# Three conditional regions per expert instead of four, with a longer ring of split weights and a shorter ring of raw ones

## The chip, the cores and the metric

One core of a Trainium2 chip runs the whole block as one program. The metric is the device time of that program in microseconds, the median of several runs. Engines: PE is the matrix engine (PEld its weight loads), DVE the vector engine, ACT the scalar engine, POOL GpSimd, SP the queue that issues most weight transfers. Some stretches depend on the data: the routing decides how many tokens each expert gets.

## The reference, cut to what matters

A transformer layer on 1024 tokens of width 1024: a mixer (gated DeltaNet beside sparse attention), an output projection, and then a routed feed-forward of 32 experts with 4 experts per token. All inputs are float32.

```python
logits = (h @ router_w + router_b)
top_val, top_idx = lax.top_k(logits, TOP_K); gate = softmax(top_val)
# for each expert e, the tokens routed to it, in blocks of 128 rows xb:
act = clamped_swiglu(xb @ w1[e] + b1[e])      # w1[e]: 1024 x 2048
y   = act @ w2[e] + b2[e]                     # w2[e]: 1024 x 1024
out[token] += gate * y
```

## The kernel before, in words

The last of four phases, `phase4`, is the expert feed-forward and takes about 1590 of the 2613 us. It is unrolled over the 32 experts. An expert's weights come as NS = 12 *pieces* of 1 MB (eight of w1, four of w2). `fetch` brings a piece into one of NR = 8 *raw* buffers (`self.raw[g % NR]`); four of them (the phase before has finished with `yT`) lie in the tile `yT`, so half of the weight transfers and splits are named `yT` in the trace. Each piece is cut into two *halves*, and `split` (lines 191 to 194) makes of each half a rounded part `hi` on ACT and the remainder `lo` on DVE, into a ring of NW = 10 buffer pairs. After the second half of a piece is split, the next transfer into that raw buffer is issued on SP (`fetch(g // 2 + NR)`).

A `Block` multiplies a block of tokens with a piece: per half, four matmuls with `hi` and `lo` against the rounded tokens, and two of `hi` against the tokens' remainder (line 1672). `behind(s)` does the work after a piece: `act` (lines 1714 to 1717, after pieces 1, 3, 5, 7), `turn` (a transpose, lines 1724 to 1729, after pieces 3, 5, 7, 9) and `result` (line 1734). Every expert has a `first` block of up to 128 tokens. If more came, a second block is computed in a conditional *region* (line 1530): `both` with all 128 rows if there are more than 192 tokens, else `half` with 64 rows, where `whole` (lines 1704 and 1705) first adds two halves of a PSUM bank into the tile `y1`, out of which the results are later added to the output by an indirect transfer (`add_rows`).

The 12 pieces are taken in groups of GP = 3: for each group its splits are issued, then the first block's three pieces, then one region with the second block's three pieces. So there are four regions per expert, 128 in all. The split issued LOOK = NW - 2 * GP = 4 halves ahead leaves room for the whole group's halves, which the region needs again:

```python
for s0 in range(0, NS, GP):
    group = range(s0, s0 + GP)
    for s in group:
        for part in range(2):
            split(2 * (e * NS + s) + part + LOOK)
    for s in group:
        first.room(s); first.piece(s, wt); first.behind(s)
    with tc.If(several > 0):
        ...
```

The order of the instructions on each engine is not the program's: a scheduler of the framework lists them by its own model of times. It takes a region as one unit on PE, ACT and DVE, and nothing is moved into or out of it; splits may end up behind a region that follows them in the program.

`phase3`, before it, loads the four pieces of `w_out` into raw[0] to raw[3], splits them into the first eight pairs of the ring (lines 1172 to 1175), and after each one issues the fetch of an expert piece into the freed buffer (line 1176). The other four raw buffers are fetched on ACT's queue near the end of the phase (line 1264).

Of the kernel before, what the change touches and what calls it, by code (L numbers as in the profile page):

```python
# [10 lines left out]
F32 = mybir.dt.float32  # L11
# [9 lines left out]
P = 128  # L21
# [6 lines left out]
NE = 32  # L28
# [10 lines left out]
ROWS = T + P  # L39
NS = 12  # L40
KEEP = 1
GP = 3
NR, NW = 8, 10
LOOK = NW - 2 * GP


# [90 lines left out]
class K:  # L137
# [1019 lines left out]
    def phase3(self):  # L1157
        nc, tc, A, pp = self.nc, self.tc, self.A, self.pp
# [4 lines left out]
        with ExitStack() as es:  # L1163
            hp = es.enter_context(self.pool("p3h", 1))
# [3 lines left out]
            self.rings()  # L1168
            wo = list(zip(self.hi, self.lo))
            wo += [tuple(hp.tile([P, 2, 512], F32R, name=f"{n}{i}") for n in ("wohi", "wolo")) for i in range(NW, 8)]  # L1170
            for g in range(4):
                nc.sync.dma_start(self.raw[g], A['w_out'][g])
            for g in range(4):
                for h in range(2):
                    self.split(self.raw[g][:, 2 * h:2 * h + 2], *wo[2 * g + h])
                self.fetch(g)
            it32 = hp.tile([P, NE], F32, name="it32")
            nc.gpsimd.iota(it32, pattern=[[1, NE]], base=0, channel_multiplier=0, allow_small_or_imprecise_dtypes=True)
            before = hp.tile([P, P], BF, name="before")
# [75 lines left out]
            for i in range(NT):  # L1255
# [3 lines left out]
                if i == NT - 2:  # L1259

                    self.raw += [self.yT[:, 2 * g:2 * g + 2].rearrange("p a (b c) -> p (a b) c", b=2) for g in range(4)]
                    with tc.issue_after(self.xload.ins):
                        for g in range(4, NR):
                            self.fetched = self.fetch(g, nc.scalar)
                if i == 0:

# [133 lines left out]
    def rings(self):  # L1400

        wp = self.wp

        self.lo = [wp.tile([P, 2, 512], F32R, name=f"lo{i}") for i in range(2)]
        self.raw = [wp.tile([P, 4, 512], F32, name=f"raw{i}") for i in range(4)]
        self.hi = [wp.tile([P, 2, 512], F32R, name=f"hi{i}") for i in range(min(NW, 8))]
        self.lo += [wp.tile([P, 2, 512], F32R, name=f"lo{i}") for i in range(2, min(NW, 8))]

# [34 lines left out]
    def phase4(self):  # L1443
        nc, tc, A, pp = self.nc, self.tc, self.A, self.pp
        ET = mybir.EngineType
        with ExitStack() as es:
            wp = es.enter_context(self.pool("moe_x"))
# [30 lines left out]
            def split(g):  # L1478
                if g < 2 * NE * NS:
                    self.split_ring(g)  # L1480
                    if g % 2:
                        self.fetch(g // 2 + NR)
# [5 lines left out]
            def gather(b, e):  # L1488
                if e < NE:
                    self.gather(self.xg[b], ix(b, e))  # L1490

            def path_of(e):
                return [nc.values_load(path[0:1, e:e + 1], engines=on, min_val=0, max_val=2)
                        for on in ((ET.PE, ET.Activation, ET.DVE), (ET.Pool,))]
# [8 lines left out]
            for e in range(NE):  # L1503
                several, pool = paths
                paths = path_of(e + 1) if e + 1 < NE else None
                pick = lambda h: self.sel[:, h, e:e + 1].to_broadcast([P, P])
                wt = lambda g: (self.hi[(2 * e * NS + g) % NW], self.lo[(2 * e * NS + g) % NW])
                first = Block(self, 0, P, self.xg[0], self.xT, pick, ga(0, e), self.y0)
                xT1 = st.tile([P, 2, KD, P], F32R, name="xT1")
                both = Block(self, 1, P, self.xg[1], xT1, pick, ga(1, e), y1)  # L1510
                half = both.half(lambda h: self.selh[:, h, e:e + 1].to_broadcast([P, P]))

                for s0 in range(0, NS, GP):
                    group = range(s0, s0 + GP)
                    if s0 == 9 and e + 1 < NE:
                        self.transpose_x(self.xg[0], self.xT)
                        gather(0, e + 2)
                    for s in group:
                        for part in range(2):
                            split(2 * (e * NS + s) + part + LOOK)  # L1520
                    if s0 == GP:
                        gather(1, e + 1)
                    for s in group:
                        first.room(s)
                        first.piece(s, wt)
                        first.behind(s)

                    for s in group:
                        both.room(s)
                    with tc.If(several > 0):  # L1530
                        with tc.If(several > 1) as many:
                            if s0 == 0:
                                self.transpose_x(self.xg[1], xT1)
                            for s in group:
                                both.piece(s, wt)
                                both.behind(s)
                        with many.Else():
                            if s0 == 0:
                                self.transpose_half(self.xg[1], half.X)
                            for s in group:  # L1540
                                half.piece(s, wt)
                                half.behind(s)
                self.add_rows(self.y0, ix(0, e), P)
                with tc.If(pool > 0):
                    self.add_rows(y1, ix(1, e), P)
# [209 lines left out]
```

## Time and profile before

| | us |
|---|---|
| median of 3 runs | 2619.31 (2616.43 to 2620.05) |
| the profiled execution's own time | 2615.12 |
| its span, first to last instruction | 2613.4 |
| PE, DVE, ACT busy in the span | 2388.0, 1953.6, 1529.1 |
| granted TensorE clock, mean | 0.968 |

Busy times are sums over instructions; those of PE overlap one another and their ends are modelled, so the distance from the start of one matmul to the start of the next tells more than its length. "Idle before <- X" names what the engine waited for. `L1530` is the line of the outer `If`; PEq, ACTq and DVEq are the engines' sequencers, which execute its branches and semaphores.

### The profile page before, as it was taken

Reading aid. Unit: us, or ns where it says so; the run is one execution under the profiler, and the core shown is the slowest. Engines: PE = TensorE matmul, PEld = TensorE weight load, DVE = VectorE, ACT = ScalarE, POOL = GpSimd, SP = SyncE. Lnnn points to the kernel's source line nnn. Section 1 sums busy time; section 2 is a strip of 40 time slices with the busy share of each in tenths; the row PEclk is TensorE's granted clock in tenths of the full one; section 3 lists DMA queues with packets and bytes.
Section 4 is the critical chain, followed back from the end, with each engine's and each line's share of the span. In section 5 each row is a group of like instructions: output and inputs, shape, how many; then the busy total and the mean of one; then the engine's idle time right before and its main releaser. Section 6 shows DMA issues by size and latency. Waiting matters only on the chain.

```text
span 2613.4 us, 35019 instructions
## 1 busy us (share of the span) xinstructions
PE 2388.0 (91%) x11702; PEld 1900.5 (73%) x11702; DVE 1953.6 (75%) x3547; ACT 1529.1 (59%) x2436; POOL 504.3 (19%) x423
## 2 busy tenths in 40 slices
PE   5999989988988896999999999799999999999986
PEld 4877768867887775777777777577777777777764
DVE  6697896388885786988787776589999867786654
ACT  6558433366765324776676665467777646664643
POOL 0033320244442333101111110120110101110100
PEclk9999999979999996999999999899999999999998
DMA  8124245554521645899695775479999857785750
GB/s 323 51 74 137 105 138 196 177 140 119 145 60 53 217 153 196 328 358 327 236 350 212 276 275 219 155 288 349 352 349 354 313 196 271 268 320 189 273 175 12
DMA packets 144836, 570.65 MB, mean 218 GB/s; under 512 B 36820, under 2 KB 62452, under 8 KB 89252
## 3 DMA queue, kind: packets, MB, share of 16 engines
q1 hardware_dynamic: 111876, 496.33, 52.3%
q0 software_dynamic: 19792, 43.37, 6.2%
q10 hardware_dynamic: 12880, 27.30, 2.9%
q8 instruction: 157, 2.57, 0.4%
q14 instruction: 131, 1.07, 0.1%
HBM read 534.89 MB, written 54.57 MB: 226 GB/s over the span
## 4 chain that ended last, share of the span: by engine, by line
issue 54%; PE 8%; POOL 5%; DMA 5%; DVE 4%; another core or an unknown queue 1%; ACT 1%; POOLq 0%; ACTq 0%; SPq 0%; DVEq 0%
POOL xg L1605 3%; DMA dL<-pair,rdest 2%; POOL out_dram L1609 2%; PE tr L1145 1%; DVE Xb L931 1%; PE big L200 1%; PE big L201 1%; PE big L202 1%; DMA raw<-in_w_out_dram 1%; PE lg L1118 1%; DMA out_dram<-y,L 1%; PE mm L1315 1%; DVE tb L929 1%; PE tr L1135 1%
## 5 line engine op out<-in xcount | busy, mean ns | idle before, releaser
L1672 PE MATMUL m<-hi,xT 128*128 128x512 f32 x2464 | 806.2, 396 | 7.7 <-DVE xT L1630 5.5
L1672 PE MATMUL m<-lo,xT 128*128 128x512 f32 x1344 | 551.9, 411 | 27.8 <-DVE lo L194 21.0
L1672 PEld LDWEIGHTS m<-hi,xT 128*128 128x128 f32 x2464 | 466.9, 190 | 112.7 <-DVE xT L1630 8.5
L194 DVE TENSOR_TENSOR lo<-raw,hi 128x1024 fp32r<-128x1024 f32 x392 | 461.4, 1219 | 38.3 <-ACT hi L193 27.4
L194 DVE TENSOR_TENSOR lo<-yT,hi 128x1024 fp32r<-128x1024 f32 x384 | 451.3, 1219 | 29.2 <-ACT hi L193 18.4
L1672 PE MATMUL m<-hi,aT 128*128 128x512 f32 x1232 | 421.2, 403 | 13.5 <-ACT aT L1728 9.5
L193 ACT CAST hi<-raw 128x1024 fp32r<-128x1024 f32 x392 | 392.6, 1048 | 31.8 <-DMA raw<-in_w_out_dram 11.9
L193 ACT CAST hi<-yT 128x1024 fp32r<-128x1024 f32 x384 | 383.9, 1047 | 17.9 <-PE m L1672 8.1
L1672 PEld LDWEIGHTS m<-lo,xT 128*128 128x128 f32 x1344 | 254.5, 189 | 133.3 <-DVE lo L194 61.9
L1672 PEld LDWEIGHTS m<-hi,aT 128*128 128x128 f32 x1232 | 231.5, 188 | 66.2 <-ACT aT L1728 12.5
L1672 PE MATMUL m<-lo,aT 128*128 128x512 f32 x672 | 267.4, 400 | 5.5 <-DVE lo L194 0.9
L1605 POOL DMA_INDIRECT xg<-dH,L x63 | 73.5, 1166 | 806.9 <-PE tr L1617 706.8
L1609 POOL DMA_INDIRECT out_dram<-y,L x41 | 108.8, 2653 | 575.3 <-DVE y L1734 490.4
L1714 ACT ACTIVATE act<-m,c 128x256 f32<-128x256 f32 x140 | 66.4, 474 | 262.1 <-PE m L1672 262.1
L1672 PEld LDWEIGHTS m<-lo,aT 128*128 128x128 f32 x672 | 126.4, 188 | 46.4 <-DVE lo L194 12.1
L200 PE MATMUL mm<-hTh,wh 128*128 128x512 f32 (+2 forms) x400 | 155.8, 390 | 1.6 <-ACT xpad L469 1.1
L201 PE MATMUL mm<-hTl,wh 128*128 128x512 f32 (+2 forms) x400 | 154.0, 385 | 0.0
L202 PE MATMUL mm<-hTh,wl 128*128 128x512 f32 (+2 forms) x400 | 154.0, 385 | 0.0
L1705 DVE TENSOR_TENSOR y<-m,y 64x512 f32<-64x512 f32 x42 | 28.6, 682 | 130.9 <-ACT y L1704 130.9
L1716 DVE TENSOR_SCALAR m<-m 128x256 f32<-128x256 f32 x140 | 59.8, 427 | 87.9 <-ACT act L1714 81.2
L1096 POOL TENSOR_TENSOR L<-Tb,mask 128x128 f32<-128x128 f32 (+3 forms) x64 | 84.9, 1327 | 161.2 <-PE tr L1135 105.9
L1728 ACT CAST aT<-tr 128x256 fp32r<-128x256 f32 (+1 forms) x168 | 59.2, 352 | 92.6 <-PE tr L1724 79.1
(460 smaller groups left out, 4123.1 us busy)
## 6 DMA issues: line engine op xcount, KB each, us to landing
raw<-in_w_dram SPq DMA_DIRECT2D x192, 1024.0 KB
yT<-in_w_dram SPq DMA_DIRECT2D x188, 1024.0 KB
raw<-in_mod_w_dram SPq DMA_DIRECT2D x24, 1024.0 KB
raw<-in_w_in_dram SPq DMA_DIRECT2D x16, 1024.0 KB
dU<-stage ACTq DMA_DIRECT2D x12, 512.0 KB
dT<-dF SPq DMA_DIRECT2D x8, 576.0 KB
x<-in_x_dram SPq DMA_DIRECT2D x8, 512.0 KB
dQK<-stage ACTq DMA_DIRECT2D x8, 512.0 KB
```

The lines of the kernel that those rows point to most:

```text
L193: nc.scalar.copy(hi, raw)
L194: nc.vector.tensor_tensor(lo, raw, hi, op=ALU.subtract)
L200: nc.tensor.matmul(ps, xh(k), yh(k), start=(k == 0), stop=False)
L201: nc.tensor.matmul(ps, xh(k), yl(k), start=False, stop=False)
L202: nc.tensor.matmul(ps, xl(k), yh(k), start=False, stop=(k == n - 1))
L1096: nc.gpsimd.tensor_tensor(L[:, :n], Tb[:, t0:t0 + n], self.masks[b], op=ALU.add)
L1605: self.nc.gpsimd.indirect_dma_start(out=xg, out_offset=None, in_=self.dH[:, :], in_offset=bass.IndirectOffsetOnAxis(ap=ix, axis=0), bounds ...
L1609: self.nc.gpsimd.indirect_dma_start(out=self.out[:, :], out_offset=bass.IndirectOffsetOnAxis(ap=ix[:z], axis=0), in_=y[:z], in_offset=None ...
L1672: mm = lambda l, r, start, stop: nc.tensor.matmul(ps, l, r, start=start, stop=stop, skip_group_check=True)
L1714: nc.scalar.activation(r, ug, AF.Relu, bias=k.c7[:z, 0:1], scale=-1.0)
L1716: nc.vector.tensor_scalar(ul, ul, 7.0, -7.0, op0=ALU.min, op1=ALU.max)
L1728: nc.scalar.copy(hi, p2)
```

## The change

GP becomes 4, NR 5 and NW 13, so LOOK becomes 5. An expert has three regions of four pieces. The transpose of the next expert's tokens moves from piece 9 to piece 8, and the gather that follows `s0 == GP` from piece 3 to piece 4. The ring of halves grows by three pairs (24 KB per partition); three of the four raw buffers outside `yT` go. Since `w_out` still needs four, three buffers `wraw` of the phase before take their place. The early fetch is that of piece 0 alone; pieces 1 to 4 are fetched into the `yT` buffers.

```diff
-GP = 3
-NR, NW = 8, 10
+GP = 4
+NR, NW = 5, 13
 LOOK = NW - 2 * GP
...
+            wraw = self.raw + [hp.tile([P, 4, 512], F32, name=f"wraw{i}") for i in range(1, 4)]
             for g in range(4):
-                nc.sync.dma_start(self.raw[g], A['w_out'][g])
+                nc.sync.dma_start(wraw[g], A['w_out'][g])
             for g in range(4):
                 for h in range(2):
-                    self.split(self.raw[g][:, 2 * h:2 * h + 2], *wo[2 * g + h])
-                self.fetch(g)
+                    self.split(wraw[g][:, 2 * h:2 * h + 2], *wo[2 * g + h])
+            self.fetch(0)
...
-                        for g in range(4, NR):
+                        for g in range(1, NR):
                             self.fetched = self.fetch(g, nc.scalar)
...
-        self.raw = [wp.tile([P, 4, 512], F32, name=f"raw{i}") for i in range(4)]
+        self.raw = [wp.tile([P, 4, 512], F32, name="raw0")]
...
-                    if s0 == 9 and e + 1 < NE:
+                    if s0 == 8 and e + 1 < NE:
```

## Rows read from the trace of the kernel before

**Rows 1.** Windows: us, busy time and count by engine, PE clock, DMA share, GB/s.
```profile
1762.00:2071.50 309.50, 303.97 (x1313) 230.34 (x1312) 281.46 (x321) 237.19 (x304) 35.02 (x24) 1.00 0.97 353
2071.50:2147.20 75.70, 74.42 (x331) 58.23 (x329) 42.14 (x57) 34.87 (x52) 4.37 (x3) 1.00 0.52 183
2147.20:2185.70 38.50, 37.79 (x165) 28.65 (x164) 35.21 (x41) 29.64 (x38) 6.46 (x4) 1.00 1.02 368
2185.70:2256.90 71.20, 65.82 (x283) 49.92 (x282) 44.03 (x62) 38.21 (x57) 5.52 (x3) 0.98 0.52 191
1218.30:1283.70 65.40, 62.68 (x282) 48.75 (x281) 43.46 (x61) 38.06 (x58) 4.36 (x3) 1.00 0.60 212
...
850.00:870.00 20.00, 14.83 (x51) 10.48 (x51) 9.64 (x9) 8.04 (x9) 5.17 (x2) 0.87 1.03 386
```

**Rows 2.** Source line 1530, whole run: count, duration ns min/median/max, first and last start.
```profile
L1530 PEldq COMPARE_BRANCH  x128: 65/220/3125, 1025.2 to 2584.1; - x128
...
L1530 PEldq EVENT_SEMAPHORE  x88: 51/51/51, 1029.5 to 2441.3; - x88
```

**Rows 3.** Groups by form, 1000 to 2613 us: busy, mean ns, idle before.
```profile
L1666 PE MATMUL m<-bias,sel 128*128 128x512 f32 x140 | 57.2, 415 | 0.0
...
L1666 PE MATMUL m<-bias,selh 128*128 128x512 f32 x28 | 11.5, 451 | 0.0
```

**Rows 4.** Timeline of PE across a skipped region: start, length, [idle before].
```profile
1840.98 0.39 PE L1672 MATMUL m<-lo,xT 128*128 128x512 f32 x1
1841.21 0.40 PE L1672 MATMUL m<-hi,xT 128*128 128x512 f32 x1
1841.76 0.47 PE L1672 MATMUL m<-lo,xT 128*128 128x512 f32 x1
1842.07 0.40 PE L1672 MATMUL m<-hi,xT 128*128 128x512 f32 x1
```

**Rows 5.** Waits of DVE, 1762 to 2071.5 us: total, times, longest.
```profile
DVE lo L194 <- ACT hi L193: 7.0, 24, 0.5
DVE lo L194 <- ACTq L1530: 5.0, 17, 0.4
DVE act L1717 <- DVEq L1530: 4.8, 14, 0.7
DVE m L1716 <- ACT act L1714: 4.3, 8, 0.6
DVE lo L194 <- DVEq L1530: 3.4, 14, 0.6
```

**Rows 6.** Timeline of PE after the second region of an expert with 64 extra rows.
```profile
1599.74 1.32 PE L1672 MATMUL m<-hi,xT 128*128 128x512 f32 x5
1603.32 0.50 PE L1672 MATMUL m<-lo,xT 128*128 128x512 f32 x1 [2.25 <-DVE lo L194]
```

**Rows 7.** Timeline of DVE in that region and after it.
```profile
1601.71 0.42 DVE L1717 SCALAR_TENSOR_TENSOR act<-y,act 64x256 f32<-64x256 f32 x1 [0.72 <-ACT act L1715]
1602.05 2.34 DVE L194 TENSOR_TENSOR lo<-yT,hi 128x1024 fp32r<-128x1024 f32 x2
```

**Rows 8.** Waits, 1630 to 1665 us, the expert after it.
```profile
ACT y L1704 <- issue: 13.1, 1, 13.1
...
PE tr L1724 <- DVE act L1717: 7.9, 1, 7.9
```

**Rows 9.** Timeline of ACT, 1786 to 1800 us: the casts of raw[0] begin the run.
```profile
1791.77 6.00 ACT L193 CAST hi<-raw 128x1024 fp32r<-128x1024 f32 x6
```

**Rows 10.** Timeline of SP, 1768 to 1800 us: issues; the first is raw[0]'s, then raw[0] again.
```profile
1770.43 10.46 SPq L1412 DMA_DIRECT2D raw<-in_w_dram  x4
...
1796.58 3.26 SPq L1412 DMA_DIRECT2D raw<-in_w_dram  x2
```

**Rows 11.** Timeline of SP, 826 to 885 us: the issue of w_out and the fetches behind it.
```profile
842.58 2.00 SPq L1172 DMA_DIRECT2D raw<-in_w_out_dram  x4
852.48 16.96 SPq L1412 DMA_DIRECT2D raw<-in_w_dram  x4
```

**Rows 12.** Timeline of ACT there: first and last cast of w_out, and its own issues.
```profile
849.02 1.99 ACT L193 CAST hi<-raw 128x1024 fp32r<-128x1024 f32 x2 [4.94 <-DMA raw<-in_w_out_dram]
...
861.96 1.05 ACT L193 CAST hi<-raw 128x1024 fp32r<-128x1024 f32 x1 [1.74 <-DMA raw<-in_w_out_dram]
...
868.90 1.04 ACT L193 CAST yh<-yT 128x1024 fp32r<-128x1024 f32 x1 [4.94 <-issue]
```

## The prediction

> **What bounds the kernel now.** I looked first at the windows of the expert phase, one expert at a time [rows 1]. Eight experts in a row that skip all their regions take 309.5 us, 38.69 us each. [...] The source view of the `If` line says how often a region is skipped: 128 branches on PE, and 88 of the semaphore instructions that only the skipping path executes [rows 2], so 22 of 32 experts skip. The groups by form give the other ten: the bias matmul of the 64-row block stands there 28 times, four per expert, so 7 experts take `half`; of the full one's 140, 128 belong to the first blocks, and 12 leave 3 experts for `both` [rows 3].
>
> Then the timeline of PE across a skipped region [rows 4]. From start to start a matmul takes 0.23 us (1840.98 to 1841.21); across the region it takes 0.55, and the one after it 0.31. A skipped region costs PE 0.32 + 0.08 = 0.40 us. The waits of DVE in the same eight experts [rows 5] show the other side: 24.5 us in these five rows, nearly all on ACT or on a sequencer at the `If`, over 32 regions 0.77 us each; DVE is idle 28.0 us in all. The splits of a group stop at the region and start again behind it, since ACT must finish its activation before it may pass with the next cast. PE then waits for `lo`. So PE and DVE pace each other, and both lose time at each region.
>
> Last, the experts with a region. A full one takes 75.7 us with PE busy 74.4; a half one late in the phase 71.2 with 65.8, an early one 65.4 with 62.7 [rows 1]. The late one's idle time is mostly a stall behind a region: PE waits 2.25 us for the first `lo` [rows 6], which DVE starts at 1602.05, right behind the second block's last activation at 1601.71 [rows 7]. The splits of the next group do not stand ahead of the region; they are made when they are needed.
>
> **The change part by part.** The sum is made against the profiled execution, 2615.12 us; the median of the runs is 4.2 us above it, and I add that at the end.
>
> *One skipped region less in 22 experts.* PE gains 0.40 us if it sets the pace, DVE 0.77 if it does. I take the middle, 0.58: 22 x 0.58 = -12.8 us. The ends are 0 (something else takes over at once) and 28.0/32 = 0.88 per region, all of DVE's idle time: -19.3. A share of 0.97 leaves the transfers room to 37.5 us per expert, and the single skipping expert at 2147.2 ran at 368 GB/s [rows 1]. So they do not cap this term.
>
> *One taken region less in 10 experts.* No row isolates its entry; PE has no drain there, the engines have their branches. Between 0 and the 0.55 of the skipped one I take 0.3: -3 us.
>
> *Late exits.* With three pieces, only the second region of an expert ends on an activation (behind piece 5; the first ends on piece 2, the third on piece 8), and the fourth on results. With four pieces the first region ends behind piece 3 and the second behind piece 7, each on an activation, the third on results. What stands queued behind that activation on DVE and ACT are the next group's splits, and PE waits for these. So the stall of rows 6 comes twice instead of once. For the five late half experts I take 2.25 less 0.45 for the small waits of the region that goes: 5 x 1.8 = +9. For the two early ones, which split further ahead, between 0 and 71.2 - 65.4 = 5.8: I take 2 each, +4. The full ones have 75.7 - 74.4 = 1.3 us idle; a second such wait is 3 x 1.3 = +4 (0 to +4).
>
> *Two half experts in a row.* There, twice in the run, ACT waited 13.1 us before it could write `y1`, whose rows were still being added to the output, and PE 7.9 us for an activation queued behind that on DVE [rows 8]. A first group of four pieces starts the region one piece later, 12 matmuls x 0.23 = 2.75 us, and the transfer ends when it did. Some of this comes back because now the transpose of the same block is in the region. Between 0 and 2 x 2.75 I take -4.
>
> *The output projection.* Four loads of `w_out` issued from 842.58 on land by 849.02 to 861.96, and three fetches follow within 17 us on the same queue [rows 11, 12], in a stretch at 386 GB/s and a share of 1.03 [rows 1]. The three that go are 3.1 MB, 8 us of transfer. ACT spends 4.94 us on issues before its next cast at 868.90 [rows 12], while PE waits for the last `w_out` halves. The gain is between 0 and, 1.74 + 4.94, 6.7 us; I take -4. The new `wraw` buffers cost nothing if they are free by 842.58, where the first load waits anyway and the others queue behind it; if not, up to 6 us of the landing time (842.58 to 849.02) is lost.
>
> *The ring of five, the earlier gather and transpose, the later fetch of pieces 1 to 3.* In a skipping expert raw[0] is issued at 1770.43, its cast starts at 1791.77 and the next issue into it is at 1796.58 [rows 9, 10]: a turn of 26.2 us for eight pieces. Five pieces make 5 x 38.69/12 = 16.1 us; less the 4.8 us from cast to issue, 11.3 are left for the landing. The first of four concurrent loads landed within 6.4 us (842.58 to 849.02) [rows 11, 12], so 4.9 us stay as cover, and I cost it at nothing. The fetch is moved past SP's small loads only, and the transpose needs tokens that were gathered an expert earlier: nothing.
>
> The sum: -12.8 - 3 + 9 + 4 + 4 - 4 - 4 = -6.8 us. That is 2608.3 for the profiled execution and, with 4.2, 2612.5 for the median.
>
> [...] The longest of the 128 branches took 3125 ns on PE, the median 220 [rows 2]. [...]
>
> **The rivals.**
>
> *The ring of five runs dry* (slower). Place: the 22 skipping experts. It decides from a landing time of 11.3 us. For it: the last of the four `w_out` loads took 842.58 to 861.96, 19.4 us, and the share is 0.97, where a queue is short of full. Against it: there four loads started at once, in the expert phase one follows a freed buffer every 3.2 us. Price: each us per expert by which the piece comes later than DVE wants it is 22 us; one us gives -6.8 + 22 = +15: 2634.
>
> *Late exits everywhere* (slower). With the shorter raw ring the two early half experts go over to the late pattern: 2 x (5.8 - 2) = +7.6; the stall at `y1` doesn't shrink, +4; the entry is free, +3. Then -6.8 + 14.6 = +8: 2627. For it: all late half experts show the pattern. Against: the early ones ran ten experts without it.
>
> *The scheduler splits ahead* (much faster, and the change as its constant LOOK = 5 reads). If five halves stand before every region, four late half experts go from 71.2 to 65.4 us, -23, the full ones lose their 1.3, -4, and no exit costs: -12.8 - 3 - 23 - 4 - 4 - 4 = -51: 2568. Against it: LOOK = 4 stands in the program now, and rows 6 and 7 show that it is not what runs.
>
> [...]
>
> **How the numbers follow.** The forecast has 0.45 (0.30 of it faster by over 0.2%, 5.2 us, which is about what a measurement of this kernel tells from no change; 0.15 within). The dry ring has 0.20 (0.17 slower, 0.03 same), late exits 0.21 (0.15 slower, 0.06 same), splitting ahead 0.12, mostly in part, the fetch 0.02. So faster 0.42, same 0.24, slower 0.34. The forecast's own range is 2600 to 2622. To hold the time 8 times in 10 it must reach to the dry ring's 2634 and, below, to the skipped regions' end (-19.3) with part of the splitting ahead: 2592.
>
> **What would show it.** A skipping expert at 38.1 us, with 66 of the skip's semaphores, DVE's waits at the `If` down by a quarter, and no wait of ACT's casts for `raw` (any there, over 0.5 us an expert, and the ring is dry). Half experts: two stalls of 2 us on `lo`, at the first and the second exit. The `y1` stall near 6 us. The last `w_out` cast before 861.96, counted from the first issue. The prediction is wrong if skipping experts stay at 38.7 us, or if the half experts change by more than 3 us.

## The result, and where the time went

The changed kernel is slower: 2630.34 us against 2616.43 (medians of 9 runs each, taken side by side), a ratio of 1.0059 with a 95% interval of 1.0045 to 1.0074. The prediction said 2612.5, faster. One experiment, with two changes to the order of the work, runs in 2567.5 us and beats both.

The profiled executions (2615.12 before, 2630.34 after) cut the difference into three stretches. The source view gives the first and last start of every line; the last matmul of the phase before (L1034), of the output projection (L202) and of the experts bound them. Of the kernel before:

```profile
L1034 PE MATMUL mm<-ident,o x32: 272/273/475, 626.9 to 842.0; 128*128 128x128 f32 x32
...
L202 PE MATMUL big<-hi,yl x128: 387/396/628, 852.0 to 975.1; 128*128 128x512 f32 x128
...
L1672 PE MATMUL m<-hi,aT x1232: 387/395/504, 1045.4 to 2593.5; 128*128 128x512 f32 x176
```

And of the changed one, with its `If` line:

```profile
L1034 PE MATMUL mm<-ident,o x32: 272/273/328, 625.8 to 839.3; 128*128 128x128 f32 x32
...
L202 PE MATMUL big<-hi,yl x128: 392/396/774, 844.3 to 962.1; 128*128 128x512 f32 x128
...
L1673 PE MATMUL m<-hi,aT x1232: 387/394/628, 1030.1 to 2608.5; 128*128 128x512 f32 x176
...
L1531 PEldq COMPARE_BRANCH  x96: 65/328/445, 1015.9 to 2597.4; - x96
...
L1531 PEldq EVENT_SEMAPHORE  x66: 51/51/51, 1020.0 to 2458.4; - x66
```

Up to L1034, where nothing was changed, one run differs from the other by 2.7 us. The projection takes 962.1 - 839.3 = 122.8 us instead of 133.1, -10.3. The experts take 1646.4 instead of 1618.4, +28.0. Sum: +15.0, of 15.2. So the change does what it says (96 branches, 66 skips), wins more ahead of the experts than predicted, and loses it twice over in them.

The windows of the experts, to be held against [rows 1]: five that skip everything, experts 5 and 8 (half, early), a full one, and two pieces of expert 5:

```profile
1775.40:1970.60 195.20, 191.31 (x822) 143.94 (x820) 175.56 (x201) 147.16 (x191) 24.25 (x15) 1.00 0.96 348
...
1219.00:1293.00 74.00, 66.46 (x282) 50.44 (x281) 44.06 (x62) 38.12 (x57) 4.42 (x3) 0.95 0.52 178
1371.50:1446.00 74.50, 66.92 (x279) 51.09 (x278) 43.60 (x61) 37.71 (x57) 4.46 (x4) 0.93 0.51 173
2088.70:2165.40 76.70, 75.05 (x330) 57.67 (x328) 41.80 (x57) 34.66 (x53) 4.49 (x3) 1.00 0.50 177
...
1271.40:1274.80 3.40, 0.44 (x3) 0.01 (x1) 3.33 (x6) 3.38 (x6) 0.00 (x0) 0.86 0.00 0
1274.80:1280.80 6.00, 6.00 (x14) 4.72 (x15) 4.81 (x5) 3.90 (x5) 0.00 (x0) 0.51 0.81 304
```

A late skipping expert takes 39.04 us (195.2 / 5), not the predicted 38.1; before it was 38.69. The early half one (expert 5) went from 65.4 to 74.0. At its end PE stood still for 3 us while no transfer ran, and then worked for 6 us at a granted clock of 0.51.

In the late skipping experts the gap that PE shows at a skipped region is what it was. PE's timeline across one, as in [rows 4], shows 0.54 us from start to start where 0.23 is usual (0.55 before):

```profile
1853.89 0.39 PE L1673 MATMUL m<-hi,xT 128*128 128x512 f32 x1
1854.43 0.47 PE L1673 MATMUL m<-lo,xT 128*128 128x512 f32 x1
```

What changed is what DVE waits for, in those five experts:

```profile
DVE lo L194 <- ACT hi L193: 8.9, 20, 0.5
DVE lo L194 <- DVEq L1531: 3.6, 15, 0.6
DVE m L1717 <- ACT act L1715: 2.8, 5, 0.6
DVE xT L1621 <- ACT xT L1620: 2.6, 5, 0.6
```

DVE's waits at the `If` fell, and by more than the predicted quarter: from (5.0 + 4.8 + 3.4) / 8 = 1.65 us per expert [rows 5] to 3.6 / 5 = 0.72. But the wait for ACT's cast rose from 7.0 / 8 = 0.88 to 8.9 / 5 = 1.78, and the copy of the tokens adds 0.52. DVE's idle time is 19.6 / 5 = 3.9 us per expert; it was 3.5. The removed wait turned into another one.

The early skipping experts lost more, most of all experts 0 to 4. In experts 1 to 4 PE waits 9.7 us in all instead of 5.0, and they take 5.1 us longer together. The largest of these waits comes once per expert, behind the third region, until DVE has passed the `If`:

```profile
PE m L1673 <- DVEq L1531: 6.5, 4, 1.7
```

Behind the third region of expert 5, PE's timeline shows the stall, and then matmuls 0.42 us apart:

```profile
1271.44 0.40 PE L1673 MATMUL m<-hi,xT 128*128 128x512 f32 x1
1274.80 0.79 PE L1673 MATMUL m<-lo,xT 128*128 128x512 f32 x1 [2.96 <-DVE lo L194]
1275.39 0.63 PE L1673 MATMUL m<-hi,xT 128*128 128x512 f32 x1
1275.81 0.63 PE L1673 MATMUL m<-lo,xT 128*128 128x512 f32 x1
```

DVE's timeline shows what it did meanwhile: the four operations of the second block's results, of which the first and the last are shown, stand ahead of the next expert's first missing half in its queue.

```profile
1270.76 0.68 DVE L1706 TENSOR_TENSOR y<-m,y 64x512 f32<-64x512 f32 x1 [3.13 <-ACT y L1705]
...
1272.86 0.74 DVE L1735 SCALAR_TENSOR_TENSOR y<-y,L,g2b 64x512 f32<-64x512 f32 x1
1273.53 4.62 DVE L194 TENSOR_TENSOR lo<-yT,hi 128x1024 fp32r<-128x1024 f32 x4
```

The 14 matmuls at the lower clock cost another 14 x 0.2 = 2.8 us (an estimate, from 0.42 us less the usual 0.23). The clock of 0.51 does not stand behind every such stall: of six of this length in `g4_ahead` below, four left it at 1.00.

SP's timeline at the start of `w_out`, against [rows 11], holds the gain; SP's wait before stands behind it:

```profile
823.79 0.46 SPq L1173 DMA_DIRECT2D raw<-in_w_out_dram  x1
832.26 5.50 SPq L1173 DMA_DIRECT2D wraw<-in_w_out_dram  x3
```

```profile
SPq L1172 <- PE mm L1034: 16.1, 1, 16.1
```

Before, the first load stood on SP for 16.1 us, until 842.58, waiting for the last matmul of the phase before; now it goes at once and the others follow 8.5 us later, so ACT casts `w_out` from 841.32 to 848.04 instead of 849.02 to 862.91.

### The profile page after: what moved, and what is told of

Read it like the earlier page. It is cut to its first block, busy times and chain, and to the rows that moved or that the text cites. A ratio compares the mean times of both kernels' runs of the same rounds, so it can differ in the third digit from the quotient of the medians.

```text
span 2628.6 us, 34659 instructions
## 1 busy us (share of the span) xinstructions
PE 2399.7 (91%) x11702; PEld 1899.0 (72%) x11702; DVE 1953.4 (74%) x3547; ACT 1525.2 (58%) x2436; POOL 541.6 (21%) x423
## 4 chain that ended last, share of the span: by engine, by line
issue 54%; PE 8%; POOL 6%; DVE 4%; DMA 4%; ACT 1%; another core or an unknown queue 1%; POOLq 0%; ACTq 0%; DVEq 0%
POOL xg L1606 3%; DMA dL<-pair,rdest 2%; POOL out_dram L1610 2%; PE tr L1145 2%; DVE Xb L931 1%; PE big L202 1%; PE big L200 1%; PE big L201 1%; PE tr L1135 1%; PE lg L1118 1%; DVE tb L929 1%; PE mm L1316 1%; DMA sc2b<-dM 1%; PE mm L1004 0%
## 5 line engine op out<-in xcount | busy, mean ns | idle before, releaser
L194 DVE TENSOR_TENSOR lo<-yT,hi 128x1024 fp32r<-128x1024 f32 x614 | 720.0, 1219 | 59.4 <-ACT hi L193 49.7
L193 ACT CAST hi<-yT 128x1024 fp32r<-128x1024 f32 x614 | 611.6, 1047 | 28.0 <-PEq L1531 15.0
L1673 PE MATMUL m<-lo,aT 128*128 128x512 f32 x672 | 276.6, 413 | 14.0 <-DVE lo L194 11.9
L1610 POOL DMA_INDIRECT out_dram<-y,L x41 | 129.0, 3147 | 656.7 <-DVE y L1735 573.2
L1606 POOL DMA_INDIRECT xg<-dH,L x63 | 89.0, 1412 | 712.9 <-PE tr L1618 534.0
L194 DVE TENSOR_TENSOR lo<-raw,hi 128x1024 fp32r<-128x1024 f32 x156 | 184.5, 1218 | 13.6 <-ACT hi L193 11.4
L1673 PEld LDWEIGHTS m<-lo,aT 128*128 128x128 f32 x672 | 128.7, 191 | 68.6 <-DVE lo L194 42.1
L193 ACT CAST hi<-raw 128x1024 fp32r<-128x1024 f32 x156 | 157.7, 1047 | 5.4 <-PEq L1531 3.1
L202 PE MATMUL mm<-hTh,wl 128*128 128x512 f32 (+2 forms) x400 | 154.0, 385 | 0.0
L1729 ACT CAST aT<-tr 128x256 fp32r<-128x256 f32 (+1 forms) x168 | 59.3, 353 | 143.8 <-PE tr L1725 122.8
```

What stands on the lines that cost most here:

```text
L193: nc.scalar.copy(hi, raw)
L194: nc.vector.tensor_tensor(lo, raw, hi, op=ALU.subtract)
L202: nc.tensor.matmul(ps, xl(k), yh(k), start=False, stop=(k == n - 1))
L1606: self.nc.gpsimd.indirect_dma_start(out=xg, out_offset=None, in_=self.dH[:, :], in_offset=bass.IndirectOffsetOnAxis(ap=ix, axis=0), bounds ...
L1610: self.nc.gpsimd.indirect_dma_start(out=self.out[:, :], out_offset=bass.IndirectOffsetOnAxis(ap=ix[:z], axis=0), in_=y[:z], in_offset=None ...
L1673: mm = lambda l, r, start, stop: nc.tensor.matmul(ps, l, r, start=start, stop=stop, skip_group_check=True)
```

## The experiments

Lengths of experts are counted from the first `If` branch on PE to that of the next expert. "Ahead" means: how many halves' casts stand on ACT ahead of each region of an expert, of the 24; the region needs its group's halves.

### Groups and rings apart

```diff
 groups3_ring5_13, on the changed kernel
-GP = 4
+GP = 3
-                    if s0 == 8 and e + 1 < NE:
+                    if s0 == 9 and e + 1 < NE:
 groups4_ring8_10, on the kernel before
-GP = 3
+GP = 4
-                    if s0 == 9 and e + 1 < NE:
+                    if s0 == 8 and e + 1 < NE:
 before_fetch_one, on the kernel before
-                self.fetch(g)
+            self.fetch(0)
-                        for g in range(4, NR):
+                        for g in range(1, NR):
```

One small thing more differs in `groups4_ring8_10`, and in `no_regions_g3`, `g3_ahead` and `g3_ring7_11_ahead` below: the early fetches are issued behind all splits of `w_out`, not one behind each piece's. Their projection takes 130.4, 131.6, 131.9 and 131.2 us instead of 133.1; the experts' lengths do not contain it.

> The changed kernel with the groups of three put back (four regions per expert, transpose back behind piece 8), and everything else of the change kept: NR 5, NW 13, w_out in wraw, one early fetch. LOOK is then 7. Theory A, that the grouping by four is what costs the expert phase its 29.6 us (first to last matmul of the experts, 1574.3 before and 1603.9 after): the phase goes back to some 1574 and the gain ahead of it stays, 2616 - 14.6 = 2602 us; skipping experts late in the run 38.7 us, the two early half experts 65 to 67. Theory B, that the ring of five raw buffers is what costs: the phase stays near 1600, 2625 to 2630 us, and the early skipping experts stand at 39 to 41 as in the changed kernel.

> The kernel before with the groups of four alone: three regions per expert, transpose behind piece 7, NR 8 and NW 10 as before, so LOOK is 2; w_out and the early fetches as before. Theory A (grouping): skipping experts 39.0 us or more and half experts 72 to 74, about 2616 + 29 = 2646 us. Theory B (ring of five): with eight raw buffers the regions pay what the prediction gave them, 38.1 us per skipping expert, and the total is about 2616 - 12 + 9 = 2613 us or less. My prediction's term for a skipped region (0.58 us) holds only in case B.

> The kernel before with one edit of the change alone: the fetches of pieces 1 to 3 behind the split of w_out go, and these pieces are fetched on ACT's queue with the others. The prediction priced this edit at -4 us (0 to -6.7). The changed kernel gains 10.4 to 11.7 us between the last load of zs and the last matmul of the output projection; 5.0 of that stands ahead of the first projection matmul (23.7 us from the issue of zs to it before, 18.7 after). Theory E, that these 5.0 come from the buffers wraw, which are free earlier than raw[0] to raw[3], and the rest from the three fetches: here the first projection matmul stays 23.7 us behind zs, the last comes 5 to 6 us earlier, and 2 to 4 of it is given back because expert 0 waits for its pieces: 2618 - 3 = 2615 us. Rival, that all comes from wraw: 2618 or more.

Groups of three with the new rings: 2608.28 us, ratio 0.9959 (0.9945 to 0.9972). Groups of four with the old rings: 2647.34, 1.0115 (1.0093 to 1.0136). The experts' stretch is 1619.4 and 1645.1 us; so theory A holds: the grouping costs some 27 us and the rings 1. It holds for the early skipping experts too: experts 0 to 4 take 190.5 us together with groups of three and the new rings, 200.6 with groups of four and the old ones (193.1 before, 203.1 in the changed kernel). Eight late skipping experts of each:

```profile
1757.40:2067.00 309.60, 303.91 (x1313) 230.40 (x1312) 281.43 (x321) 237.13 (x304) 35.03 (x24) 1.00 0.97 351
```

```profile
1781.80:2097.90 316.10, 304.30 (x1313) 230.52 (x1312) 276.59 (x320) 230.64 (x304) 40.38 (x24) 1.00 0.94 345
```

38.70 us with three and five raw buffers, exactly as before with eight; 39.51 with four and eight raw buffers, and its early half experts are at 71.7 and 71.6. The ring of five is not dry, and theory B falls.

The fetches alone: 2615.0 us, 0.9989 (0.9976 to 1.0003), no change that can be told; the projection takes 129.3 us (842.3 to 971.6), 3.8 less. So of the 10.3 us, 3.8 are the fetches, as priced, and by difference 6.5 the new buffers. Theory E holds in its order, with 3.8 and 6.5 for its 5 to 6 and 5.

### What a skipped region costs

Both kernels without second blocks, one run each:

```diff
-                    for s in group:
-                        both.room(s)
-                    with tc.If(several > 0):
...
                 self.add_rows(self.y0, ix(0, e), P)
-                with tc.If(pool > 0):
-                    self.add_rows(y1, ix(1, e), P)
```

> The kernel before (NR 8, NW 10, groups of three; w_out in raw) with the second blocks left out in the same way. If a skipped region costs 0.40 to 0.88 us: 38.69 - 4 x 0.58 = 36.4 us per expert (37.1 to 35.2). If regions only take the place of waits that come anyway: 38.3 us or more, and the same as the one with groups of four, since without regions the groups set only the order in which splits are listed.

> The changed kernel with the second blocks left out (the conditional regions, their gather by tokens beyond 128 stays, their results are not added), so that all 32 experts run like skipping ones but without any region. If a skipped region costs what I priced, 0.40 to 0.88 us: an expert takes 39.04 - 3 x 0.58 = 37.3 us (37.8 to 36.4). If the regions only take the place of waits that come anyway because DVE, ACT and PE wait for each other at each activation: 38.5 us or more.

Eight late experts, first of the kernel before without regions, then of the changed one:

```profile
1661.70:1964.40 302.70, 299.44 (x1313) 232.33 (x1312) 277.58 (x321) 233.73 (x304) 62.10 (x16) 1.00 0.97 356
```

```profile
1649.40:1951.20 301.80, 299.19 (x1313) 232.34 (x1312) 277.59 (x321) 232.04 (x304) 54.01 (x16) 1.00 0.98 356
```

37.84 and 37.73 us. Four regions cost 38.69 - 37.84 = 0.85, 0.21 each; three cost 39.04 - 37.73 = 1.31, 0.44 each. The prediction's price fails with four regions (36.4 expected, 37.1 at most) and is at the edge of its range with three (37.8 to 36.4); the rival's 38.3 and 38.5 did not come either. The larger part of what an expert takes over PE's own work is there without any region. PE's own work is seen in experts 5 to 9 of the kernel before without regions: there 13 to 10 casts stand ahead of an expert's first activation (6 in the late ones), and PE is busy throughout, at 35.94 us each:

```profile
1263.30:1443.00 179.70, 179.70 (x821) 146.38 (x820) 167.59 (x199) 142.47 (x189) 17.90 (x10) 1.00 0.98 372
```

In the eight late ones the engines wait for each other four times per expert, once at each activation, with no region there:

```profile
ACT act L1699 <- PE m L1657: 51.5, 32, 3.9
PEld m L1657 <- DVE lo L194: 17.4, 48, 0.4
DVE lo L194 <- ACT hi L193: 14.1, 32, 0.5
```

### The order of the splits

From the eleventh to thirteenth expert on, the scheduler's lists change by themselves: before, 10, 16, 20 and 28 halves stand ahead of the four regions in the first experts and 7, 13, 19 and 25 later; after, 13, 21 and 27, later 9, 17 and 25, just the region's own and one. Three kernels force the splits ahead (`self.cast` and `self.rest` are the two instructions of the last split; the second of them also has NR, NW = 7, 11), one moves the activation, one the transpose:

```diff
 g3_ahead (kernel before), g3_ring7_11_ahead, g4_ahead (changed kernel)
-                        first.behind(s)
+                        with tc.issue_after(self.cast.ins), tc.issue_after(self.rest.ins):
+                            first.behind(s)
 g4_act_behind_region, on the changed kernel
-                        first.behind(s)
+                        if s < group[-1]:
+                            first.behind(s)
...
                             for s in group:
                                 half.piece(s, wt)
                                 half.behind(s)
+                    first.behind(group[-1])
 g4_x_behind_splits, on the changed kernel
-                    if s0 == 8 and e + 1 < NE:
-                        self.transpose_x(self.xg[0], self.xT)
-                        gather(0, e + 2)
...
                     for s in group:
+                        if s == 8 and e + 1 < NE:
+                            self.transpose_x(self.xg[0], self.xT)
+                            gather(0, e + 2)
```

> The kernel before (groups of three, NR 8, NW 10) with one thing added: each activation and turn of the first block is queued on ACT and DVE behind the last split of its group, so that the halves split ahead stay at 10, 16, 20 and 26 casts before the four regions to the end; in the kernel before, they fall to 7, 13, 19 and 25 from the eleventh expert on. Theory C, that the 65 us of the early half experts against 71 later come from this head start alone: the half experts 10, 12, 13, 25 and 31 lose about 5 us each, the skipping ones stay at 38.7, total 2619 - 25 = 2594 us. Rival, that the late half experts are slower for another reason (transfers, the clock): 2619 us within 0.2%.

> The same with NR 7 and NW 11: three raw buffers outside yT, so that one of the four loads of w_out goes into a buffer wraw, and three early fetches instead of four; groups of three. If the early start of w_out in the changed kernel comes from the buffers of wraw, a part of its 14.6 us comes back here, some 8 us of it after the first expert has waited longer for its pieces: 2594 - 8 = 2586 us. If it needs all three wraw buffers: 2594. If C is wrong: 2611 or more.

2632.72 us, 1.0057 (1.0039 to 1.0075), and 2641.89, 1.0091 (1.0073 to 1.0109). Theory C falls: the late half experts 10, 12 and 25 fell to 68 to 70, but the late skipping ones rose. Five late ones of g3_ahead and an early one:

```profile
1839.70:2044.50 204.80, 195.06 (x822) 149.59 (x821) 173.37 (x201) 145.04 (x191) 24.06 (x15) 0.96 0.89 331
...
1281.40:1320.10 38.70, 37.16 (x166) 29.10 (x165) 34.65 (x42) 29.11 (x39) 9.42 (x4) 1.00 0.97 364
```

40.96 us, with the clock at 0.96: a PE stall of 1.3 us in each, and PE idle for (204.80 - 195.06) / 5 = 1.95 us. The same stall left the clock at 1.00 in experts 14 and 15, which take 39.8 with PE idle for 2.1.

> The changed kernel with the same order forced: 13, 21 and 27 casts before its three regions to the end (9, 17 and 25 from the thirteenth expert on without it). Theory C2, that with groups of four the head start does not help, because the first halves behind the third region are split behind the results on DVE in any case: half experts 12, 13, 25, 31 go from 71 to 74 us, skipping ones stay at 39.0 to 39.3, 2630 + 12 = 2642 us. Rival, that the early experts of the changed kernel are slow for what the start of the phase does (late first pieces): half experts 71, 2630 us or less.

2640.99 us, 1.0096 (1.0078 to 1.0115). The total is C2's, but it came otherwise. PE's stall of 2.94 to 2.96 us behind the third region now stands in half experts 5, 8, 10, 12, 13 and 25, as C2 said; yet only 10 and 12 rose, to 75.8 and 74.5, with the clock at 0.93 and 0.95. In the other four it stayed at 1.00 and they take 71.1 to 71.6, less than in the changed kernel. The skipping ones are at 357.4 / 9 = 39.71, above C2's 39.0 to 39.3. Nine of these, expert 12 and expert 5:

```profile
1745.30:2102.70 357.40, 337.12 (x1478) 259.73 (x1477) 310.80 (x361) 259.93 (x342) 47.01 (x28) 1.00 0.91 343
1599.20:1673.60 74.40, 66.58 (x282) 50.65 (x281) 44.10 (x62) 37.90 (x57) 4.43 (x3) 0.95 0.51 180
1223.40:1294.70 71.30, 63.81 (x281) 48.45 (x280) 43.89 (x62) 38.04 (x57) 4.41 (x3) 1.00 0.52 189
```

> The changed kernel with the transpose of the next expert's tokens put behind the splits of its group in the program (still ahead of piece 8), so that its copies on ACT and DVE no longer stand ahead of them: the lists then hold 13, 21 and 29 halves ahead of the three regions on ACT and on DVE, in all experts (before this: 13, 21, 27 and 25, and from the thirteenth expert on 9, 17, 25 and 8, 16, 24). That is the rival 'the scheduler splits ahead' of the prediction, now made to run. If the head start is what the exits lack: the stall of 3.1 us on lo behind the third region of the early half experts goes, half experts 65 to 68 us, six of them by 5 us, skipping ones at 38.3 to 39, some 2630 - 30 = 2600 us. If splits in a lump ahead of the regions cost as much in the skipping experts as they did when I forced them (39.7 in g4_ahead): 2630 to 2640.

2692.37 us, 1.0293 (1.0269 to 1.0317). The rival "splits ahead" in full is the slowest of all. PE waits for the tokens' copy, which ACT makes behind seven casts in a row (PE's timeline, then ACT's):

```profile
1832.74 0.50 PE L1673 MATMUL m<-hi,xT 128*128 128x512 f32 x1 [2.81 <-ACT xT L1620]
```

```profile
1825.47 6.73 ACT L193 CAST hi<-yT 128x1024 fp32r<-128x1024 f32 x7
1832.11 1.06 ACT L1620 CAST xT<-tr 128x512 fp32r<-128x512 f32 x2
```

> The changed kernel with the work behind the last piece of each group of the first block (activation and turn behind pieces 3 and 7, a result behind piece 11) placed behind the region instead of ahead of it. Theory D, that a skipped region costs more with groups of four because it stands directly behind an activation, so that ACT and DVE pass it late: skipping experts go from 39.04 to 38.3 us or less, -0.7 x 22 = -15, 2615 us. Rival, that it costs what PE's own gap costs (0.39 us) wherever it stands: 39.0 us, 2630.

2605.25 us, 0.9953 (0.9936 to 0.9970): faster, but not by theory D as it was meant. The late skipping experts stay at 312.5 / 8 = 39.06; the gain is in the first experts, in which splits are still ahead (experts 1 to 4 take 151.3 us together instead of 160.0, and PE has no wait in 1 and 2), and in the early half ones (72.0 and 70.7 instead of 74.0 and 74.5). So in the early experts the work right ahead of a region does count; at the third one it is the first block's results. Windows of the eight and of expert 2:

```profile
1764.10:2076.60 312.50, 305.52 (x1312) 229.54 (x1312) 279.59 (x321) 231.99 (x305) 41.67 (x24) 1.00 0.97 349
1095.10:1131.80 36.70, 36.25 (x165) 28.93 (x164) 34.31 (x41) 30.01 (x41) 8.43 (x3) 1.00 1.01 396
```

### The results at the exit

```diff
-        if s == 11 or s == 10 and self.b == 0:
+        if self.b == 0 and s in (10, 11):
```

> The changed kernel with the results of the second blocks left out (the two reads of PSUM on ACT, two sums and two products on DVE behind piece 11; what is added to the output for them is old data). Theory F, that the early half experts of the changed kernel take 74 us because the first half that PE wants behind the third region is split on DVE behind these results (PE idle 2.96 us, and matmuls 0.43 us apart instead of 0.23 for 6 us after it): the stall of 3.1 us goes to under 1, experts 5 and 8 take 68 to 70 us, the later half ones lose the 1.87 us behind their third region, the total 2630 - 15 = 2615 us. Rival, that the splits wait for the transfers there: the stall stays over 2 us.

2606.41 us, 0.9963 (0.9947 to 0.9979). Expert 5 without the second blocks' results (expert 8 takes 68.6):

```profile
1223.80:1293.20 69.40, 64.94 (x282) 49.57 (x281) 41.29 (x58) 36.86 (x55) 4.41 (x3) 0.98 0.54 194
```

No PE stall over 1 us is left at that exit. Theory F holds, for 4.6 and 5.9 us of the early half experts' 8; the total fell by more than expected, as the late ones 12 and 25 got 3.5 shorter too. The run takes away the work with its place in the queue, so it doesn't tell the two apart.

### Both together, and with four, no and other regions

The activation behind the region and the other activations behind the splits, in groups of four, then with GP = 3, without regions, and with NR, NW = 6, 12:

```diff
-                        first.behind(s)
+                        if s < group[-1]:
+                            with tc.issue_after(self.cast.ins), tc.issue_after(self.rest.ins):
+                                first.behind(s)
...
+                    first.behind(group[-1])
```

> The kernel g4_act_behind_region (work behind the last piece of a group placed behind the region) with the first block's other activations and turns queued behind the splits of their group, which keeps 11, 21 and 26 casts ahead of the regions to the end, about the lists of its experts 1 and 2, which took 37.0 and 36.7 us. Theory G, that an expert takes 37 us where both hold, splits ahead and no activation at the region: skipping experts 37.0 instead of 39.05, 18 x -2.0 = -36, 2605 - 36 = 2570 us. Rival, that the first experts were fast because full raw buffers had gathered by then: 39 us or more, 2605 or more.

> The kernel g4_act_behind_region_ahead (2567.5 us) with groups of three, so four regions per expert; same rings (NR 5, NW 13), same early w_out, the work behind the last piece of a group behind its region, the rest of it behind the splits of its group. Theory H, that the prediction's first term holds once the splits stand ahead of the region and no activation stands right before it, because then PE sets the pace and a region costs what PE loses on it (0.31 + 0.08 = 0.39 us): skipping experts 37.55 + 0.39 = 37.9 us, the total 2567 + 22 x 0.4 and some for the ten others, 2577 to 2583 us. Rival, that grouping by four is a loss in any order (0.35 us per skipping expert, and the half experts): 37.2 us, 2555 us.

> The kernel g4_act_behind_region_ahead with the second blocks left out (no regions, results of the second blocks not added). Theory H: its three regions cost 3 x 0.39 = 1.2 us of the 37.55 per skipping expert, so 36.4 us here. Rival, that something else (a transfer, DVE) stands at 37.5: 37.5 us.

> The kernel g4_act_behind_region_ahead with NR 6 and NW 12 (LOOK 4; two raw buffers outside yT, two wraw, two early fetches): 10, 20 and 26 casts ahead of the regions. If the ring of five is dry now that the splits run ahead: 2567 - 10 = 2557 us. If five are enough and the fifth half ahead is used: 2570 us or more; a part of w_out's early start may go too, as two fetches stand ahead instead of one (+2).

| | us | ratio to before (95%) | late skipping expert |
|---|---|---|---|
| groups of four, both | 2567.49 | 0.9816 (0.9796 to 0.9837) | 300.6 / 8 = 37.58 |
| groups of three, both | 2608.50 | 0.9967 (0.9951 to 0.9982) | 308.5 / 8 = 38.56 |
| four, both, no regions | (2232.48, without second blocks) | | 288.2 / 8 = 36.03 |
| four, both, ring 6 and 12 | 2617.81 | 0.9998 (0.9986 to 1.0009) | 309.7 / 8 = 38.71 |

The windows, in the table's order:

```profile
1747.90:2048.50 300.60, 295.64 (x1314) 231.82 (x1313) 277.81 (x322) 232.74 (x305) 36.35 (x24) 1.00 0.98 361
```

```profile
1755.80:2064.30 308.50, 298.55 (x1314) 230.46 (x1313) 274.47 (x321) 230.11 (x304) 69.31 (x24) 1.00 0.96 353
```

```profile
1635.70:1923.90 288.20, 288.20 (x1313) 234.34 (x1312) 274.07 (x321) 230.27 (x305) 26.79 (x16) 1.00 1.00 374
```

```profile
1772.60:2082.30 309.70, 297.52 (x1313) 231.79 (x1312) 276.86 (x321) 228.08 (x303) 58.58 (x25) 1.00 0.96 351
```

Theory G holds (2570 expected). Neither half of it moves a late skipping expert down alone (39.06 and 39.71 against 39.04); together they take 1.5 us off. In this order PE sets the pace (without regions it is busy for 288.2 of 288.2 us), and regions cost what H said or more: three of them 37.58 - 36.03 = 1.55 us, 0.52 each. With four the expert takes 0.98 more, and the total 41 us; the lists of these two differ in more than the region (13, 19, 22 and 28 halves ahead with four), so not all of it is the region's. And LOOK = 5 counts: with one pair less and one raw buffer more, PE waits 8.4 us in the eight experts for the first half behind a region, against 1.4 for `lo` with 13 pairs. These are PE's whole lists of waits, ring 6 and 12 first:

```profile
PE m L1677 <- DVEq L1534: 8.4, 8, 1.1
PE m L1677 <- DVE lo L194: 1.4, 8, 0.2
```

```profile
PE m L1676 <- DVE lo L194: 1.4, 8, 0.2
```

Of the 50 us between these two kernels, 8 lie in the output projection (129.6 us with two buffers `wraw`, 121.5 with three). The ring of five is short, though, in the fast kernel: ACT's casts wait 16.5 us for transfers in its eight experts, four times the sign that the prediction set for a dry ring (0.5 us an expert), and 0.4 us with six raw buffers. PE feels little of it there, as the 1.4 us show; a ring of six with 13 pairs was not run.

```profile
ACT hi L193 <- DMA yT<-in_w_dram: 13.9, 22, 2.2
ACT hi L193 <- DMA raw<-in_w_dram: 2.6, 6, 0.6
```

## Why the prediction was wrong

Between the two profiled executions, by the prediction's steps:

| step | predicted | measured |
|---|---|---|
| skipped regions, 22 experts | -12.8 | +21.8 (the eight up to expert 9: +13.4, expert 11: +2.1, the 13 later ones: +6.3) |
| taken regions (ten experts), late exits (five half experts): measured in half experts 10, 12, 25 | -3, +9 | -3.4, +1.4, +1.2: -0.8 |
| two early half experts | +4 | +16.3 |
| full experts | +4 | +3.5 |
| `y1`, half after half | -4 | stall 7.9 to 3.6 in expert 13, which got 7.6 shorter; in the last expert 5.5 to 2.1 |
| output projection | -4 | -10.3 |

The rest is -2.7 ahead of all this and -5.0 at both ends of the expert phase, where the first branch now stands one piece later; it holds the last expert's `y1`. The entry of a taken region is short in the trace of the kernel before: PE's starts lie 0.32 us apart there (1222.16 to 1222.48 us, expert 5) against 0.55 across a skipped one, and drains stand on PE only at 0.3 us and from 2594.2 us on.

- **The step that failed is "One skipped region less in 22 experts".** It took the idle time seen at the regions for the regions' price. Without regions the late experts still take 37.8 us: PE, ACT and DVE wait for each other at each activation, as the waits without regions show (in eight experts ACT 51.5 us for PE, PE's weight loads 17.4 for `lo`, DVE 14.1 for ACT's casts), because ACT makes the next cast only behind it; with the activations queued behind the splits and no regions, the expert takes 36.03. In the order that the two kernels have, a region costs 0.21 us in groups of three, and the longer groups raise it to 0.44. Why these 0.23 us more, I have not shown: the activation next to the region is not it (39.06). In the early experts the work right ahead of the region (an activation, at the third region the results) is a part: the eight skipping experts up to expert 9 lost 13.4 of the 21.8 us, and putting that work behind the region gave 8.8 back in experts 1 to 4. Why expert 0 alone takes 4.9 us more is not shown.
- The gain was real but conditional. With splits ahead and no activation at the region, a region costs 0.52 us, near the 0.58 of the prediction; the change came without that order.
- *Two early half experts* failed by size. The prediction saw the second exit; the third, behind the results, was not in it, nor the clock of 0.51 behind it (0.95 and 0.93 over experts 5 and 8). The late half ones had a stall behind the results before as well, and there the term was right: half experts 12 and 25 rose by 1.4 and 1.2 us, for 1.8 - 0.3 = 1.5 predicted.
- The full experts and the fetches were right (3.5 and 3.8 for 4 and 4). That `wraw` costs nothing was too cautious: it gains 6.5. The `y1` term was too small as well: the two stalls got 4.3 and 3.4 us shorter, where the prediction allowed 2.75 each at most.
- The rivals. The ring of five: not dry in this change, by the sweep above and because ACT's casts wait for no transfer in the late skipping experts. Splits ahead: slower, not faster, when done alone. The fetch, with its chance of 0.02, was the author's estimate for a skipped region that costs as much as the longest branch lasts (3125 ns [rows 2]), and no run shows it: on PE a branch that skips takes 330 ns in the median in both kernels and one that enters its region 70, so the medians 220 [rows 2] and 328 are two mixtures, and a longer jump takes no longer. The kernel before has not one long branch but four, of 1930, 2060, 3097 and 3125 ns, all at a third region early on; the changed kernel has none over 445. Nor were they a price: while the one of 3125 ns ran, from 1197.19 us, PE's matmuls followed each other 0.23 us apart. Late exits everywhere: half right; experts 5 and 8 did worse than the late pattern, not like it. That its 2627 us came near is luck: it had the skipped regions at -12.8 and no gain at `y1`.

## What to carry to other kernels

Idle time that stands next to a construct is not the construct's price (0.40 us of PE and 0.77 of DVE stood at a skipped region here, and it cost 0.21): take it out altogether and time what is left, before pricing one less of it. Where the queues of ACT and DVE shared splits, activations and conditional regions, what stood right ahead of and behind a region decided here: two changes of order that each left a skipping expert as it was (39.06 us for 39.04) or made it slower (39.71) were worth 1.5 us per expert together (37.58). A look-ahead in the program is only what the scheduler makes of it: count in the trace how much stands ahead of each region, early and late in the run.

## What the hardware showed beside it

In expert 5 of the changed kernel a stall of 2.96 us cost nearly twice its length (the 2.8 us estimated above on top), as PE then ran for 6.0 us at a granted clock of 0.51. But the same stall passed without it elsewhere: in `g4_ahead` half experts with a stall of 2.94 to 2.96 us took 71.1 to 71.6 us with the clock at 1.00, and 74.5 and 75.8 where it was 0.95 and 0.93 in the mean. In `g3_ahead` skipping experts with a stall of 1.3 us took 39.8 us at 1.00 and 40.96 at 0.96. So experts with the same stalls in one run differed by 1 to 4 us here, and a comparison of two orders needs several experts.
